# A reshape, tile and logsumexp kernel: the x buffers moved by 96 bytes, to a multiple of 4096

## The chip, the cores and the metric

The kernel runs on one core of a Trainium2 chip. Such a core has five engines with instruction streams of their own: TensorE (PE) for matmuls, VectorE (DVE), ScalarE (ACT), GpSimd (POOL) and SyncE (SP), which here issues transfers. Sixteen DMA engines move data between DRAM and the core's on-chip memory, which has 128 partitions. The metric is the time of one execution on the device in microseconds, as the median of several runs.

## What is computed

The input x has the shape (8, 2048, 2048) in float32, 134 MB. Its last dimension is cut into 8 heads of 256 columns. A bias of 256 values per head is added, and the logarithm of the sum of exponentials is taken over each head's 256 columns. Each result stands twice in the output, of shape (8, 8, 4096).

```python
def reference(x, bias):
    B, S, D = x.shape
    H = bias.shape[0]
    Dh = D // H
    x_heads = x.reshape(B, S, H, Dh).transpose(0, 2, 1, 3)
    x_heads = x_heads + bias[None, :, None, :]
    x_tiled = np.repeat(x_heads, 2, axis=2)
    mx = x_tiled.max(axis=-1, keepdims=True)
    lse = mx.squeeze(-1) + np.log(np.exp(x_tiled - mx).sum(axis=-1))
    return lse.astype(np.float32)
```

## The kernel before

x is worked through in 64 tiles of 256 rows of the sequence: 128 partitions with K = 2 rows of 2048 columns each, 2 MB a tile. The kernel takes exponentials without subtracting a maximum first; at the end a small judgement over all sums decides whether a slower loop (`all_again`) is needed, which runs only for extreme data.

**Buffers.** All tiles of on-chip memory come out of one pool, `sb`, which hands out places in the order in which the code asks for them, each at a multiple of 32 bytes (lines 155 to 201). First come the bias and its copies, among them `b_rep` (line 156, the bias of heads 4 to 7 in every partition) and `w_sb` (line 157), then the sums `R`, then the results `res`, `res_two` and `res_last` (lines 195 to 200), and last the four buffers `xb0` to `xb3` (line 201). Each of the four holds KB = 4 rows of 2048 float32 per partition, 32,768 bytes. `xts` (line 202) cuts them into eight places for a tile.

**Loads.** SP issues all loads of x, in the order of the program. The first two tiles come one by one (line 276). Tiles 2 to 41 come in pairs, one transfer of 4 MB into a whole buffer, in which each partition receives 32 KB in one piece (line 261). From tile 42 on each tile has its own transfer again, with 16 KB in one piece per partition, or 8 KB in the last batch, where a partition's two rows lie apart in DRAM. Tiles from 57 on are loaded row by row, 1 MB each, and the last two tiles in ten parts of 1 to 8 heads (`TAIL_LOADS`, line 54). A load into a buffer waits for the last uses of what stood there (`last_uses`, collected per tile); `reload` (line 289) issues it.

**Work on a tile.** Most tiles go by the split `BULK`. PE adds the bias to heads 0 to 2 (line 464: x times the identity on top of the bias in PSUM), and ACT takes their exponentials from there (lines 475 and 482). POOL adds the bias to heads 4 to 7 in place (line 514, `g_add`), ACT takes the exponentials of heads 3 to 7 (line 520), and DVE multiplies head 3 by the exponential of its bias (line 532) and sums all heads but the first in one reduction (line 539). The last tiles use other splits, and the last two follow an order written out by hand (`TAIL`, line 71): there PE adds the bias per piece (line 846) and runs small matmuls between (line 455) whose results aren't used. The order of the instructions on every engine is that of the program; no scheduler moves them.

The functions that the change touches are printed here; it stands among the tiles of the kernel's own function.

Of the kernel before, what the change touches and what calls it, by code (L numbers as in the profile page):

```python
# [9 lines left out]
F32 = mybir.dt.float32  # L10
# [114 lines left out]
def kernel(  # L125
# [7 lines left out]
    P = nc.NUM_PARTITIONS  # L133
# [16 lines left out]
    sb = ctx.enter_context(tc.tile_pool(name="sb", bufs=1))  # L150
# [47 lines left out]
    ]  # L198
    res_two = sb.tile([H * NBLK, P, K, 2], F32, name="res_two")
    res_last = sb.tile([P, P, 2], F32, name="res_last")  # L200
    xbs = [sb.tile([P, KB, D], F32, name=f"xb{i}") for i in range(NBUF // TB)]
    xts = [xb[:, k : k + K] for xb in xbs for k in range(0, KB, K)]
    w_ps = pp.tile([P, W2 - W0], F32, name="w_ps")
# [100 lines left out]
    for set_idx, (_name, funcs) in enumerate(get_activation_tables(nc.m.arch).items()):  # L304
        if ACT.Exp in funcs and ACT.Ln in funcs:
            nc.scalar.add_instruction(
                mybir.InstLoadActFuncSet(
                    name=nc.get_next_instruction_name(),
# [707 lines left out]
```

## Time and profile before

| | |
|---|---|
| median of 3 runs | 325.6 us (325.59 to 325.68) |
| the profiled execution's own time | 325.55 us |
| its span, from the first to the last instruction | 323.7 us |
| granted TensorE clock, mean | 0.961 |
| read from DRAM, written | 134.23 MB, 1.05 MB |
| DMA packets | 8806 |

The span is shorter than the execution by what lies before the first and after the last instruction. In the rows over time the span is cut into 40 equal slices, and each digit is a busy share in tenths. A row of a group reads: line, engine, operation, what it writes and reads with shapes, the count, then busy time in us and the mean of one in ns, then the engine's idle time just before, and what ended it. In the rows of a DMA queue stand packets, MB, and the time that the packets took as a share of the 16 DMA engines' time; rows of single transfers give their size in KB and the median time from issue to landing.

### The profile page before, as it was taken

The numbers are of one execution on the slowest core, as the hardware profiler recorded it, in microseconds if no ns is written. First come the engines' busy times: TensorE is split into PE (matmuls) and PEld (weight loads), VectorE is DVE, ScalarE is ACT, GpSimd is POOL, SyncE is SP. The second block draws the span as 40 slices with busy tenths as digits, with TensorE's granted clock in tenths as the row PEclk, the third lists the DMA queues.
The fourth block names the chain that finished last, engine by engine and source line by source line (L and its number), as shares of the span: only waits on it lengthen the run. The fifth ranks groups of instructions, "written<-read, shape, count | busy, mean of one in ns | idle before, by whom it ended". The sixth has DMA issues, their size and how long they took to land.

```text
span 323.7 us, 2296 instructions
## 1 busy us (share of the span) xinstructions
PE 247.5 (76%) x619; PEld 100.1 (31%) x620; DVE 288.0 (89%) x310; ACT 265.6 (82%) x436; POOL 287.9 (89%) x119
## 2 busy tenths in 40 slices
PE   5997787688776698886668878677778678688775
PEld 1332332233332233332223323233233322233333
DVE  1339998889999969999999998999999999989985
ACT  1169868878778869688889869878988999999995
POOL 7949997999999999999999999999999999878783
PEclk9999979899999879799999979999999999799999
DMA  7999999999999999999999999999999999999993
GB/s 309 470 397 445 454 401 440 445 409 441 445 409 442 441 407 441 441 413 438 445 410 441 441 411 441 413 427 427 433 429 422 429 424 426 419 421 419 419 399 145
DMA packets 8806, 135.44 MB, mean 418 GB/s; under 512 B 980, under 2 KB 1239, under 8 KB 2519
## 3 DMA queue, kind: packets, MB, share of 16 engines
q1 hardware_dynamic: 8640, 135.14, 98.2%
q10 hardware_dynamic: 152, 0.14, 0.1%
q8 instruction: 5, 0.08, 0.1%
q14 instruction: 9, 0.07, 0.1%
HBM read 134.23 MB, written 1.05 MB: 418 GB/s over the span
## 4 chain that ended last, share of the span: by engine, by line
DMA 58%; POOL 18%; ACT 14%; PE 5%; DVE 3%; SPq 1%; issue 0%
DMA xb<-in_x_dram 58%; POOL xb L514 18%; ACT xb L520 9%; DVE R L539 2%; PE pair L464 2%; ACT xb L495 2%; ACT xb L482 1%; PE one_ps L464 1%; ACT xb L475 1%; PE pair L846 1%; PE tp L455 1%; SPq L261 1%; DVE xb L532 0%; SPq L276 0%; PE pair L826 0%
## 5 line engine op out<-in xcount | busy, mean ns | idle before, releaser
L514 POOL TENSOR_TENSOR xb<-xb,b_rep 128x2048 f32<-128x2048 f32 x57 | 256.7, 4527 | 21.2 <-DMA xb<-in_x_dram 21.2
L539 DVE TENSOR_REDUCE R<-xb 128x14 f32<-128x3584 f32 (+1 forms) x57 | 216.8, 3803 | 3.4 <-ACT xb L520 1.5
L520 ACT ACTIVATE xb<-xb 128x2560 f32<-128x2560 f32 (+5 forms) x80 | 156.2, 1965 | 20.1 <-POOL xb L514 19.5
L464 PE MATMUL pair<-xb,ident 128*128 128x512 f32 x216 | 108.2, 625 | 0.0
L464 PE MATMUL one_ps<-xb,ident 128*128 128x512 f32 x108 | 62.9, 667 | 20.2 <-DMA xb<-in_x_dram 20.2
L482 ACT ACTIVATE xb<-pair 128x1024 f32<-128x1024 f32 x54 | 55.3, 1025 | 17.4 <-PE pair L464 17.3
L464 PEld LDWEIGHTS pair<-xb,ident 128*128 128x128 f32 x216 | 44.1, 204 | 58.1 <-issue 58.1
L532 DVE TENSOR_TENSOR xb<-xb,w_ps 128x512 f32<-128x512 f32 x54 | 36.7, 680 | 21.2 <-ACT xb L520 21.2
L406 PE MATMUL one_ps<-b,ones_bf 128*128 128x512 bf16 x52 | 19.9, 382 | 38.0 <-ACT xb L475 38.0
L475 ACT ACTIVATE xb<-one_ps 128x256 f32<-128x256 f32 x108 | 39.8, 375 | 6.8 <-PE one_ps L464 6.8
L406 PEld LDWEIGHTS <-ones_bf 128*128 128x128 bf16 (+1 forms) x174 | 17.3, 100 | 85.4 <-issue 78.5
L406 PE MATMUL pair<-b,ones_bf 128*128 128x512 bf16 x104 | 31.0, 379 | 0.0
L464 PEld LDWEIGHTS one_ps<-xb,ident 128*128 128x128 f32 x108 | 19.6, 200 | 35.7 <-DMA xb<-in_x_dram 29.8
L441 PE MATMUL pair<-xb,ident 128*128 128x512 f32 x32 | 18.6, 684 | 8.5 <-DMA xb<-in_x_dram 8.5
L555 DVE CUSTOM_DVE_ANT_0 xb<-xb,w_ps 128x256 f32<-128x256 f32 x60 | 22.1, 413 | 0.4 <-ACT xb L520 0.4
L475 ACT ACTIVATION_READ_ACCUMULATOR xb<-one_ps 128x1 f32 x108 | 21.8, 202 | 0.0
L578 POOL TENSOR_TENSOR xb<-xb 128x128 f32<-128x128 f32 (+3 forms) x36 | 13.5, 379 | 2.5
L495 ACT ACTIVATE xb<-pair 128x256 f32<-128x256 f32 x38 | 14.4, 395 | 1.0 <-PE pair L846 0.7
L572 POOL TENSOR_TENSOR xb<-xb,w_sb 128x256 f32<-128x256 f32 (+1 forms) x12 | 10.1, 840 | 4.3 <-ACT xb L520 3.7
L455 PE MATMUL tp<-b_rep,ident 128*128 128x384 f32 x30 | 12.0, 486 | 0.0
L441 PEld LDWEIGHTS pair<-xb,ident 128*128 128x128 f32 x32 | 5.3, 197 | 17.7 <-DMA xb<-in_x_dram 15.9
L495 ACT ACTIVATION_READ_ACCUMULATOR xb<-pair 128x1 f32 x38 | 8.4, 220 | 0.0
(66 smaller groups left out, 84.0 us busy)
## 6 DMA issues: line engine op xcount, KB each, us to landing
xb<-in_x_dram SPq DMA_DIRECT2D x20, 4096.0 KB, 22.6
xb<-in_x_dram SPq DMA_DIRECT2D x17, 2048.0 KB, 22.7
xb<-in_x_dram SPq DMA_DIRECT2D x11, 1024.0 KB, 22.8
xb<-in_x_dram SPq DMA_DIRECT2D x5, 256.0 KB, 9.9
xb<-in_x_dram SPq DMA_DIRECT2D x2, 512.0 KB, 17.6
xb<-in_x_dram SPq DMA_DIRECT2D x1, 640.0 KB
out_dram<-res SPq DMA_DIRECT2D x1, 512.0 KB
out_dram<-res SPq DMA_DIRECT2D x1, 256.0 KB, 5.5
```

Source lines behind the costliest of these rows:

```text
L406: nc.tensor.matmul(p, lhsT=lhsT, rhs=each_row(b, h * Dh, Dh, K), start=i == 0, stop=False,)
L441: mm = nc.tensor.matmul(p, lhsT=ident, rhs=xts[t % NBUF][:, ka:kb, c : c + w], start=False, stop=True,)
L455: nc.tensor.matmul(tp[:, 0 : WARM // P], lhsT=ident, rhs=b_rep[:, 0:WARM], start=True, stop=True)
L464: mm = nc.tensor.matmul(p, lhsT=ident, rhs=xts[t % NBUF][:, :, h * Dh : (h + 1) * Dh], start=False, stop=True,)
L475: act = nc.scalar.activation(out=xts[t % NBUF][:, k, 0:Dh], in_=got[0][:, k * Dh : (k + 1) * Dh], func=ACT.Exp, accum_out=sums[:, k, 0:1],)
L482: act = nc.scalar.activation(out=xts[t % NBUF][:, :, Dh : m["pe"] * Dh].rearrange("p k (h j) -> p h k j", j=Dh), in_=got[-1].rearrange("p ...
L495: act = nc.scalar.activation(out=xts[t % NBUF][:, k, h * Dh : (h + 1) * Dh], in_=p, func=ACT.Exp, accum_out=sums[:, k, h : h + 1],)
L514: add = nc.gpsimd.tensor_tensor(out=v, in0=v, in1=each_row(b_rep, c - G0, D - c, k1 - k0), op=ALU.add)
L520: return on_x(t, nc.scalar.activation(out=v, in_=v, func=ACT.Exp), [after])
L532: mul = nc.vector.tensor_tensor(out=f, in0=f, in1=each_row(w_ps, m["pe"] * Dh - W0, n, k1 - k0), op=ALU.mult,)
L539: red = nc.vector.tensor_reduce(out=sums[:, k0:k1, h0:H], in_=v.rearrange("p k (h j) -> p k h j", j=Dh), op=ALU.add, axis=mybir.AxisListTy ...
L555: ttr = nc.vector.tensor_tensor_reduce(out=v, in0=v, in1=w, scale=1.0, scalar=0.0, op0=ALU.mult, op1=ALU.add, accum_out=dst,)
```

## The change

A tile of 24 float32, 96 bytes per partition, is asked of the pool between `res_last` and the x buffers. Nothing writes or reads it.

```diff
     res_two = sb.tile([H * NBLK, P, K, 2], F32, name="res_two")
     res_last = sb.tile([P, P, 2], F32, name="res_last")
+    sb.tile([P, 24], F32, name="gap")
     xbs = [sb.tile([P, KB, D], F32, name=f"xb{i}") for i in range(NBUF // TB)]
     xts = [xb[:, k : k + K] for xb in xbs for k in range(0, KB, K)]
```

In the built programs `res_last` stays at byte 60,320 of each partition, and the four buffers, 32,768 bytes apart, begin at byte 61,440 in place of 61,344. All other tiles stay where they were. The order of the instructions on each engine, their shapes and their waits are the same; the lines after 200 count one higher.

## The prediction

> **What bounds the kernel now.** I read first the page's head, with the busy time of each engine, and the rows over time for the DMA engines.
>
> ```profile
> span 323.7 us, 2296 instructions
> ...
> PE 247.5 (76%) x619; PEld 100.1 (31%) x620; DVE 288.0 (89%) x310; ACT 265.6 (82%) x436; POOL 287.9 (89%) x119
> ...
> DMA  7999999999999999999999999999999999999993
> GB/s 309 470 397 445 454 401 440 445 409 441 445 409 442 441 407 441 441 413 438 445 410 441 441 411 441 413 427 427 433 429 422 429 424 426 419 421 419 419 399 145
> ...
> q1 hardware_dynamic: 8640, 135.14, 98.2%
> ```
>
> No compute engine is above 89%, while the queue that loads x keeps the 16 DMA engines busy for 98.2% of the span. From the second slice to the last but one the DMA row stands at 9. The rate sinks a little towards the end, from some 430 to 420 GB/s; that slope is used below. Next come the chain of work that ended last and the DMA queue's own waits.
>
> ```profile
> DMA 58%; POOL 18%; ACT 14%; PE 5%; DVE 3%; SPq 1%; issue 0%
> ```
>
> ```profile
> SPq L261 <- DVE R L539: 177.1, 17, 27.2
> ```
>
> The loads hold 58% of the chain. SP waits 177.1 us for VectorE to free buffers, but that wait costs nothing as long as earlier transfers in the queue fill the DMA engines, and the DMA row says they do. The chain gives 18% to POOL, so I compared POOL's own pace with the loads'.
>
> ```profile
> L514 POOL TENSOR_TENSOR xb<-xb,b_rep 128x2048 f32<-128x2048 f32 x57 | 256.7, 4527 | 21.2 <-DMA xb<-in_x_dram 21.2
> L539 DVE TENSOR_REDUCE R<-xb 128x14 f32<-128x3584 f32 (+1 forms) x57 | 216.8, 3803 | 3.4 <-ACT xb L520 1.5
> ```
>
> A tile of x is 2,097,152 bytes; at the 431 GB/s measured below it takes 4.87 us to arrive. POOL's addition takes 4.53 us a tile and is itself kept waiting by the loads for 21.2 us in all. So the DMA engines set the pace and POOL has 7% in hand. Last, the end of the chain in order of time:
>
> ```profile
> 299.82 14.39 DMA xb<-in_x_dram
> 314.21 0.04 issue
> 314.26 0.70 PE pair L846 x2
> ...
> 320.81 0.15 DVE verdict L681
> ```
>
> The work after the last awaited load begins at 314.26 us and has 9.4 us to the span's end. It is short work on landed data, so it moves with the stream: a microsecond saved on the loads is a microsecond saved at the end.
>
> **The change, part by part.** It adds a tile that no instruction names: no instruction, no DMA, no wait. The order on every engine stays. The buffers of x move from byte 61,344 of each partition to byte 61,440, which is 15 times 4096. The old start lies 160 bytes past a multiple of 256 and 96 bytes short of one of 4096; the four buffers are 32,768 bytes apart, so all share this offset. Two costs could change: the DMA engines' time for a row, and the compute engines' time on x.
>
> **The DMA engines' time for a row.** Each partition's contiguous run is one packet, as the counts show: the loads have these sizes,
>
> ```profile
> xb<-in_x_dram SPq DMA_DIRECT2D x20, 4096.0 KB, 22.6
> xb<-in_x_dram SPq DMA_DIRECT2D x17, 2048.0 KB, 22.7
> xb<-in_x_dram SPq DMA_DIRECT2D x11, 1024.0 KB, 22.8
> xb<-in_x_dram SPq DMA_DIRECT2D x5, 256.0 KB, 9.9
> xb<-in_x_dram SPq DMA_DIRECT2D x2, 512.0 KB, 17.6
> xb<-in_x_dram SPq DMA_DIRECT2D x1, 640.0 KB
> ...
> xb<-in_x_dram SPq DMA_DIRECT2D x1, 128.0 KB, 14.4
> ```
>
> and 57 loads of 128 rows, with 128 more because tile 56 takes two separate rows per partition, make 7,424 rows: 464 for each of the 16 engines. Three stretches of the DMA view hold rows of one length each, 32, 16 and 8 KB: 20 to 200 us, 218 to 262 us and 277 to 300 us, in this order.
>
> ```profile
> DMA packets 2675, 77.55 MB, mean 431 GB/s; under 512 B 304, under 2 KB 304, under 8 KB 304
> q1 hardware_dynamic: 2668, 77.46, 100.1%
> ```
>
> ```profile
> DMA packets 1294, 18.85 MB, mean 428 GB/s; under 512 B 143, under 2 KB 143, under 8 KB 143
> q1 hardware_dynamic: 1292, 18.83, 100.6%
> ```
>
> ```profile
> DMA packets 1317, 9.68 MB, mean 421 GB/s; under 512 B 135, under 2 KB 135, under 8 KB 135
> q1 hardware_dynamic: 1316, 9.68, 101.3%
> ```
>
> The packets under 512 B mark completions; the rest of q1's are rows. The engines are full throughout, so a row costs 16 engines times the stretch over its rows: 16 x 180 / 2364 = 1.2183 us, 16 x 44 / 1149 = 0.6127 us, 16 x 23 / 1181 = 0.3116 us. Doubling the row from 16 to 32 KB adds 0.6056 us, which is 27.06 bytes per ns; from 8 to 16 KB it adds 0.3011 us, or 27.2. What doesn't grow with length is 2 x 0.6127 - 1.2183 = 7.1 ns by the longer pair and 2 x 0.3116 - 0.6127 = 10.5 ns by the shorter, with each row's share of completions in it. Over 464 rows that is 3.3 to 4.9 us. Alignment can act on this part alone, so 4.9 us bounds a gain: 320.7 us.
>
> How much of it comes from the odd start? No row shows a load into an aligned buffer. The nearest row is the last store, alone on the DMA engines at the end (321 to 323.7 us). It writes rows of 1 KB to DRAM, not to a row of x.
>
> ```profile
> q10 hardware_dynamic: 144, 0.13, 14.3%
> ...
> out_dram<-res_last ACTq DMA_DIRECT2D x1, 128.0 KB, 1.8
> ```
>
> Its 128 rows and 16 completions took 14.3% of 16 x 2.7 us, or 6.18 us; the bytes account for 131,072 / 27.06 = 4.84 us, and 1.33 us over 144 packets is 9.3 ns each. Counted the same way, completions included, the loads' 7.1 to 10.5 ns a row (9 packets per 8 rows) are 6.3 to 9.3 ns a packet. Loads begin oddly where they write and the store begins oddly where it reads (its source, res_last, lies at byte 60,320, also 160 past a multiple of 256); both have the same fixed time. So a fixed time of this size belongs to any packet, and I take nothing for the odd start. Bounds: a gain of 4.9 us as above; on the other side the nearest row is again the fixed part, paid once more if aligned rows were treated worse, 3.3 us at its lower value, 328.9 us.
>
> [...]
>
> **The compute engines' time on x.** PE, ACT, DVE and POOL do the same instructions 96 bytes further on. The loads hide them: POOL's 4.53 us stands under 4.87 us. If that cover went, each per cent on POOL's addition beyond the 7% would cost 0.045 x 57 = 2.6 us. No row shows the addition at another offset; the nearest is POOL's small subtraction on other tiles:
>
> ```profile
> L327 POOL TENSOR_TENSOR brest<-brow,bparts 1x768 f32<-1x768 f32 x1 | 1.6, 1627 | 0.1
> ```
>
> It takes 1627 / 768 = 2.12 ns an element against 4527 / 2048 = 2.21 for the addition, at unlike offsets. A move of 4% between offsets stays under the cover. I take nothing.
>
> **Sum.** The profiled execution took 325.55 us, 1.85 us of it outside the span; the median of the three runs is 325.6. With zero for both terms, 325.55 stays, and beside the median 325.6 us.
>
> **Rivals.** First, the odd start does cost on the write side: the piece of 160 bytes in front of every row is carried as if it were data. For it: 160 / 27.06 = 5.9 ns fits inside the fixed 7.1 to 10.5 ns. Against it: the store, and that it would leave only 1.2 ns at the lower value for all else. Its price is 464 x 5.9 ns = 2.7 us, 322.9 us; the stream would still be the bound, since a gain of 0.9% doesn't use up POOL's 7%. [...]
>
> Second, a smaller piece goes away: one broken-up write per row, priced by the unexplained spread of the fixed part, 10.5 - 7.1 = 3.4 ns, 1.6 us in all: 324.0 us. For it stands that something in the fixed part differs between stretches; against it, that the stretches have the same offset.
>
> Third, on the other side: with all rows beginning on the same boundary, the writes of the 16 engines and the accesses of the compute engines to x fall on the same pieces of memory more often. Its place is the row, its price 0.46 us for each ns a row; it decides (passes 0.65 us) from 1.4 ns, and at the spread of 3.4 ns it gives 327.2 us. For it: the rate already varies between slices, from 397 to 454 GB/s in the first ten. Against it: the buffers have a common offset now as well. [...]
>
> Fourth, the change does nothing because the buffers don't move: the placement in the built program excludes it, so it adds only to no change.
>
> **How the numbers follow.** No change 0.45 (with the fourth), the 160 bytes 0.18, the smaller piece 0.15, the collisions 0.22. A difference of 0.2%, 0.65 us, is about what a measurement here can tell from none. So faster 0.33, same 0.45, slower 0.22. The likeliest case's own range is 325.0 to 326.2; the range that takes in both signs runs from 322.6, just under the first rival, to 327.2.
>
> **What would show it.** Right: the rates of the three stretches stay at 431, 428 and 421 GB/s, the addition at 4527 ns, the last awaited load at 314.2 us. First rival: a row costs 5.9 ns less in every stretch, so that the 8 KB stretch reaches 429 GB/s and the 32 KB one 432.5. Third: those rates fall, most for short rows. I am wrong if the time moves with the rates unchanged, for then the start or the tail made it, or if POOL's addition passes 4.87 us.

## The result, and the profile after

The changed kernel takes 323.6 us (323.49 to 323.71 over 6 runs) beside 325.63 us for the kernel before (325.59 to 325.78, 6 runs). The ratio is 0.9937 with an interval of 0.9924 to 0.9950: 2.0 us faster. The time lies inside the range that was given, which took in both signs; the direction, no change, was not right.

The page's head, the rows over time of the DMA engines and the group of POOL's addition, for the changed kernel:

```profile
span 321.8 us, 2297 instructions
...
PE 249.2 (77%) x620; PEld 101.1 (31%) x620; DVE 287.5 (89%) x310; ACT 264.4 (82%) x436; POOL 288.9 (90%) x119
...
DMA  7999999999999999999999999999999999999993
...
q1 hardware_dynamic: 8640, 135.14, 98.2%
...
L515 POOL TENSOR_TENSOR xb<-xb,b_rep 128x2048 f32<-128x2048 f32 x57 | 257.6, 4549 | 19.1 <-DMA xb<-in_x_dram 19.1
```

The DMA engines are full as before and for the same 98.2% of a span that is 1.9 us shorter, with the same packets and bytes. The compute engines do what they did; POOL's addition is 4549 ns in place of 4527. So the DMA engines got through the same rows sooner. The end of the chain in order of time:

```profile
298.26 14.05 DMA xb<-in_x_dram
312.31 0.04 issue
312.36 0.70 PE pair L847 x2
```

The work after the last awaited load begins at 312.36 us, it was 314.26: the whole 1.9 us is there when the last load lands, and the tail behind it is as long as it was. The chain's shares changed more than the time (DVE has 27% of it now, it had 3%). With SP waiting for VectorE (177.5 us at L262, 79.9 us at L277) as well as for transfers (28.2 us at L277), the chain can go back through either; the DMA row says that the engines stayed full all along (9 from the second slice to the last but one).

The three stretches of the DMA view with rows of 32, 16 and 8 KB, 20 to 200 us, 218 to 262 us and 277 to 300 us:

```profile
DMA packets 2684, 77.84 MB, mean 432 GB/s; under 512 B 304, under 2 KB 304, under 8 KB 304
q1 hardware_dynamic: 2677, 77.76, 100.1%
```

```profile
DMA packets 1304, 19.00 MB, mean 432 GB/s; under 512 B 144, under 2 KB 144, under 8 KB 144
q1 hardware_dynamic: 1302, 18.97, 100.8%
```

```profile
DMA packets 1339, 9.81 MB, mean 427 GB/s; under 512 B 141, under 2 KB 141, under 8 KB 141
q1 hardware_dynamic: 1338, 9.81, 101.0%
```

By the prediction's own arithmetic a row now costs 16 x 180 / 2373 = 1.2137 us, 16 x 44 / 1158 = 0.6079 us and 16 x 23 / 1197 = 0.3074 us: 4.6, 4.8 and 4.2 ns less than before, whatever the row's length. Over the 464 rows of an engine that makes 1.9 to 2.2 us, which is the gain.

The trace also records how long each packet took, though not on which engine; where rows of an engine are counted below, they are a sixteenth of all. These are the commonest durations of the load queue's rows, in ns with their counts, and the mean, before and after (counted from the trace's packets):

```
rows of 32 KB  before  1213 x657, 1214 x548, 1218 x389, 1221 x338   mean 1217.5
               after   1213 x2543 of 2560                          mean 1214.1
rows of 8 KB   before  311 x471, 314 x246, 312 x154, 313 x137       mean 314.3
               after   309 x1661 of 1664                            mean 309.3
```

Before, a row took its shortest time or some ns more, in several steps; after, nearly every row takes the shortest time. The changed kernel's stream has lost a spread that for most rows was 0 to 12 ns. From about its 6th row to its 31st each engine takes the shortest time before the change too. The experiments ask what boundary the price hangs on, whose it is, and why these first rows don't pay it. Below, a row is called odd when its start in on-chip memory is not a multiple of 256 bytes, and even when it is.

### The profile page after: what moved, and what is told of

Read it like the earlier page. It is cut to its first block, busy times and chain, and to the rows that moved or that the text cites. A ratio compares the mean times of both kernels' runs of the same rounds, so it can differ in the third digit from the quotient of the medians.

```text
span 321.8 us, 2297 instructions
## 1 busy us (share of the span) xinstructions
PE 249.2 (77%) x620; PEld 101.1 (31%) x620; DVE 287.5 (89%) x310; ACT 264.4 (82%) x436; POOL 288.9 (90%) x119
## 3 DMA queue, kind: packets, MB, share of 16 engines
q1 hardware_dynamic: 8640, 135.14, 98.2%
## 4 chain that ended last, share of the span: by engine, by line
DMA 54%; DVE 27%; PE 6%; ACT 6%; POOL 4%; SPq 1%; issue 0%
DMA xb<-in_x_dram 54%; DVE R L540 23%; ACT xb L521 4%; POOL xb L515 4%; DVE xb L533 4%; PE pair L465 3%; PE one_ps L465 2%; ACT xb L483 1%; PE pair L847 1%; PE tp L456 1%; DVE R L635 1%; ACT xb L476 0%; SPq L262 0%; SPq L277 0%; PE pair L827 0%
## 5 line engine op out<-in xcount | busy, mean ns | idle before, releaser
L515 POOL TENSOR_TENSOR xb<-xb,b_rep 128x2048 f32<-128x2048 f32 x57 | 257.6, 4549 | 19.1 <-DMA xb<-in_x_dram 19.1
L465 PE MATMUL pair<-xb,ident 128*128 128x512 f32 x216 | 110.2, 636 | 0.0
L465 PEld LDWEIGHTS pair<-xb,ident 128*128 128x128 f32 x216 | 45.0, 208 | 59.0 <-issue 59.0
L442 PE MATMUL pair<-xb,ident 128*128 128x512 f32 x32 | 18.4, 676 | 8.0 <-DMA xb<-in_x_dram 7.9
L442 PEld LDWEIGHTS pair<-xb,ident 128*128 128x128 f32 x32 | 5.4, 196 | 16.6 <-DMA xb<-in_x_dram 14.8
```

The costliest lines, as they stand in the source:

```text
L442: mm = nc.tensor.matmul(p, lhsT=ident, rhs=xts[t % NBUF][:, ka:kb, c : c + w], start=False, stop=True,)
L465: mm = nc.tensor.matmul(p, lhsT=ident, rhs=xts[t % NBUF][:, :, h * Dh : (h + 1) * Dh], start=False, stop=True,)
L515: add = nc.gpsimd.tensor_tensor(out=v, in0=v, in1=each_row(b_rep, c - G0, D - c, k1 - k0), op=ALU.add)
```

## Experiments

### Which boundary

Against the changed kernel, only the size of the unused tile differs, so that x begins 32 bytes short of a multiple of 64, and on odd multiples of 64, 128 and 256.

```diff
-    sb.tile([P, 24], F32, name="gap")
+    sb.tile([P, 16], F32, name="gap")   # start_32; 40, 56 and 88 columns in the other three
```

> The x buffers begin at byte 61,408, 32 bytes short of a multiple of 64 (and of 4096). Theory A (a row that doesn't begin on some boundary pays a few ns more on its DMA engine): 325.3 to 325.9 us, the rates of the 32, 16 and 8 KB stretches as before the change (431, 428, 421 GB/s). Rival B (it is the move that counts, away from a chance collision between x and the other tiles, not the boundary): near 323.6 us.

> The x buffers begin at byte 61,504, a multiple of 64 and not of 128. Theory A with a boundary of 64 bytes: 323.6 us, the 8 KB stretch at 427 GB/s. Theory A with a boundary of 128 or more: 325.6 us and 421 GB/s. Rival B (a chance collision of places): anything between 323.6 and 325.6 us, out of order with the other starts.

> The x buffers begin at byte 61,568, a multiple of 128 and not of 256. Theory A with a boundary of 64 or 128 bytes: 323.6 us; with a boundary of 256 or more: 325.6 us. Rival C (the boundary is 4096, as the change has it): 325.6 us.

> The x buffers begin at byte 61,696, a multiple of 256 and not of 512. Theory A with a boundary of at most 256 bytes: 323.6 us, packets of 8 KB rows as in the changed kernel, 8 KB stretch at 427 GB/s. Rival C (the boundary is 4096): 325.6 us and 421 GB/s.

| start | past a multiple of 256 by | us, median | ratio to before, interval |
|---|---|---|---|
| 61,408 | 224 | 326.18 | 1.0013, 1.0004 to 1.0023 |
| 61,504 | 64 | 325.75 | 1.0002, 0.9992 to 1.0012 |
| 61,568 | 128 | 325.65 | 0.9996, 0.9986 to 1.0005 |
| 61,696 | 0 | 323.72 | 0.9941, 0.9924 to 0.9957 |

The 8 KB stretch (277 to 300 us) of the start at 128 and of the one at 256:

```profile
q1 hardware_dynamic: 1317, 9.68, 101.3%
```

```profile
q1 hardware_dynamic: 1338, 9.81, 101.1%
```

A multiple of 128 gains nothing, a multiple of 256 has the full gain. The 4096 in the change's name is not needed, and theory A holds with a boundary of 256 bytes. Rival B, a chance collision with other tiles, would not sort these starts. What I hadn't put in any expectation is the first row of the table: 224 bytes past a boundary is a little slower than the 160 of the kernel before (8 KB rows: mean 315.1 ns against 314.3).

### The loads alone

A kernel of its own brings x in through four buffers in rows of 8 KB, 1024 rows for each DMA engine. Sums, exponentials and the output's values are left out. Its loop, shortened:

```python
for i in range(B * n):
    xb = xbs[i % 4]
    nc.sync.dma_start(out=xb, in_=rows)    # rows: x[b, 512 rows] as "(k p) d -> p k d"
    nc.vector.tensor_copy(seen[:, i : i + 1], xb[:, 0, 0:1])
```

> Loads alone: x is brought in through four buffers at byte 61,344 and so on, all in rows of 8 KB, and of each load one column is copied so that the buffer is used before it is filled again; sums, exponentials and the output's values are left out (zeros are written). Theory A1 (the price is the DMA engines' own): a row costs 3 to 6 ns more than in the run with buffers at 61,440, over 1024 rows an engine 3 to 6 us, some 320 against 316 us. Theory A2 (odd rows collide with the compute engines' accesses to x, for which these are gone): no difference within 0.5 us.

> The same loads alone into buffers at byte 61,440 and so on. Both theories: the 8 KB rows go at 427 GB/s, as in the changed kernel's 8 KB stretch, some 316 us. A1: 3 to 6 us below the run with odd buffers; A2: within 0.5 us of it.

With buffers at 61,344 it took 328.27 us, with buffers at 61,440 it took 323.76 us, one run each. The absolute times were expected 8 us too low (I had counted the rows' own time and little else); the difference, 4.5 us, is within what A1 said. The DMA view from 20 to 300 us, odd buffers and then even:

```profile
DMA packets 14873, 118.17 MB, mean 422 GB/s; under 512 B 448, under 2 KB 448, under 8 KB 448
q1 hardware_dynamic: 14873, 118.17, 101.4%
```

```profile
DMA packets 15101, 119.91 MB, mean 428 GB/s; under 512 B 464, under 2 KB 464, under 8 KB 464
q1 hardware_dynamic: 15101, 119.91, 101.0%
```

14,425 and 14,637 rows in 280 us are 310.6 and 306.1 ns a row: 4.5 ns for an odd start. VectorE was busy for 2% of this span and PE and ACT not at all, so the price is no collision with the compute engines' accesses.

In this run, too, the first rows are free. In the trace's packets the price sets in near row 38 of each engine, some 14 us after the start; in the kernel before it sets in near row 42, some 43 us after the start, since most of its rows there are four times as long. Between these two runs it is the count of rows that agrees, not the time.

### Half of the buffers

Against the changed kernel, the four buffers are asked for one by one, with 160 unused bytes between the second and the third (the lines that matter):

```diff
+        if i == 2:
+            sb.tile([P, 40], F32, name="gap2")
         xbs.append(sb.tile([P, KB, D], F32, name=f"xb{i}"))
```

> Buffers xb0 and xb1 begin on a multiple of 256, xb2 and xb3 160 bytes past one, as all four did before. Theory A (every row with an odd start pays its own price): half of the gain, 324.6 us, and two kinds of rows side by side. Rival D (one odd stream disturbs all, so that the DMA engines lose step with each other): little of the gain, 325.2 to 325.7 us.

324.35 us, ratio 0.9959 (0.9945 to 0.9973): 70% of the gain, by the time nearest to theory A. But the rows don't bear A out. The 8 KB stretch stands at the full rate although half of its buffers are odd:

```profile
q1 hardware_dynamic: 1337, 9.81, 101.1%
```

and of the 2560 rows of 32 KB, 2441 take the shortest 1213 ns, where half of them should have been slower. Neither theory had said so: odd rows among even ones are nearly free. Most of what was still paid lies in the last part, where tiles 62 and 63 are loaded in pieces into `xb3` alone, an odd buffer (the 5 KB rows take 200.5 ns on average, as before, against 196.0 in the changed kernel). What the packets took beyond the shortest times adds up to some 0.4 us an engine more than in the changed kernel, of the 0.7 us between the two kernels. Together with the free first rows this suggested some slack in each DMA engine that takes up the price of some 40 odd rows and is given back by even ones. The next run was made for that.

> Loads alone as before, but two buffers begin 160 bytes past a multiple of 256 and two on one, so that each DMA engine gets 64 odd rows of 8 KB, then 64 even ones, and so on; sums, exponentials and the output's values are left out. In the run with odd buffers alone the first 37 rows or so of each engine cost nothing and all later ones some 5.5 ns. Theory S (an odd row's price is first taken up by some slack in the engine, and even rows give the slack back): prices only in the second half of each odd run, 324.4 to 325.2 us. Theory P (each odd row pays for itself): half of the way between the two runs, 326.0 us. Theory D (once the engines have lost step, odd rows pay from then on): 325.8 to 326.0 us, with clean rows in even runs alone.

Against the loads alone with odd buffers (the lines that matter):

```diff
+        if i == 2:
+            sb.tile([P, 24], F32, name="gap")
         xbs.append(sb.tile([P, KB, D], F32, name=f"xb{i}"))
```

324.93 us (one run), inside what theory S gave and 1 us below the other two. The DMA view of this run from 4 to 12 us (odd rows, early), 92 to 100 us (odd rows, late in a run of 64) and 62 to 90 us (even rows and the first odd ones after):

```profile
DMA packets 416, 3.41 MB, mean 426 GB/s; under 512 B 0, under 2 KB 0, under 8 KB 0
...
DMA packets 413, 3.38 MB, mean 423 GB/s; under 512 B 0, under 2 KB 0, under 8 KB 0
...
DMA packets 1498, 12.00 MB, mean 429 GB/s; under 512 B 33, under 2 KB 33, under 8 KB 33
```

In the packets of the same run nearly all rows from 62 to 90 us take 309 ns, and from 92 to 100 us most take 311 to 321 ns; this pattern comes back with each turn through the buffers. After the first turn some 32 of the 64 odd rows are free each time. So slack is the reading that foretold the number. What the slack is made of no run shows.

### Which side, which end

Loads alone again, into even buffers, with rows cut to 8032 bytes, so that a row has one broken piece of 96 bytes beside 31 whole blocks of 256.

```diff
-        nc.sync.dma_start(out=xb, in_=rows)
+        nc.sync.dma_start(out=xb[:, :, 0:2008], in_=rows[:, :, 40:2048])   # cols_src
```

(`cols_00` reads columns 0 to 2007 and writes them there; `cols_both` reads and writes 40 to 2047.)

> Loads alone, rows cut to 8032 bytes, read from the start of each 8 KB row in DRAM and written to the start of an even row: starts even on both sides, ends odd. The last 40 columns of each row and all of the arithmetic are left out. If ends cost nothing: 160 bytes less for each of 1024 rows an engine is 6.0 us below the 323.8 us of whole even rows, 317.7 us. If an odd end costs like an odd start: about 322 us.

> The same, read from 160 bytes into each row in DRAM, written to an even start; the first 40 columns and the arithmetic are left out. Theory W (only the written start counts): as the run with even starts on both sides. [...] Theory M (read and written starts must match modulo 256): 4 to 6 us more.

> The same with both starts 160 bytes past a multiple of 256; the first 40 columns and the arithmetic are left out. Theory W: 4.5 us more than the run with even starts on both sides, as whole odd rows stand to whole even ones. [...] Theory M: no more than it.

They took 320.69, 320.57 and 320.75 us, one run each: all alike, and 3 us above the 317.7 us that was worked out for rows without a price. An odd read start alone (`cols_src`) cost nothing against the other two, and theory M falls, since starts that differ were no dearer than starts that match. Theory W falls in the form I had given it, for it expected 4.5 us between the last and the first. What the three have in common is one broken block a row where they write, at its end or at its start. Their rows from 20 to 300 us, the same in all three within three packets:

```profile
q1 hardware_dynamic: 15247, 118.74, 101.3%
```

The reads were broken at one end at least in all of them, so one thing stayed open, and two runs settled it: rows of 31 whole blocks, written whole, and read either from the row's start or from 160 bytes into it.

```diff
+        nc.sync.dma_start(out=xb[:, :, 0:1984], in_=rows[:, :, 40:2024])   # blocks_src; 0:1984 in blocks_even
```

> Loads alone, rows cut to 7936 bytes, 31 blocks of 256, even starts and ends on both sides; the last 64 columns and the arithmetic are left out. No broken block anywhere: 256 bytes less for each of 1024 rows an engine is 9.6 us below whole even rows, 314.1 us, and no slower rows late in the run.

> The same, but read from 160 bytes into each row in DRAM, so that reads begin and end inside a block and writes don't; 64 of the columns and the arithmetic are left out. Theory W (only broken writes cost): 314.1 us as the other. Theory R (an odd read start carries the 160 bytes in front): 6.0 us more. Reads priced like writes: 4.5 us more.

314.21 and 313.97 us, one run each, where 314.1 was expected of both if only broken writes cost. A price for the second run's reads of 6.0 us (theory R) or of 4.5 us doesn't show. From 20 to 300 us, reads from a row's start and then from inside it:

```profile
q1 hardware_dynamic: 15579, 119.83, 101.2%
```

```profile
q1 hardware_dynamic: 15581, 119.84, 101.2%
```

Broken reads from DRAM are free here: 313.97 us against 314.21. (No trace shows where x begins in DRAM; the two reads lie 160 bytes apart, so at least one of them starts inside a block.) Broken writes into on-chip memory cost 2.8 ns for one piece of 96 bytes a row (320.69 us against 317.8, which is 314.21 us plus 96 bytes at 27.06 bytes per ns for 1024 rows, over 1024 rows) and 4.5 ns for the two pieces, 96 and 160 bytes, that an odd row of whole blocks breaks into.

One estimate fits both prices, though no run was made to test it: each block that a row touches where it writes costs a fixed 4.5 ns beside the time of its bytes. An odd row of 8 KB touches 33 blocks in place of 32 and pays 4.5 ns more. A cut row touches 32 blocks for the bytes of 31.375, and 0.625 x 4.5 = 2.8 ns. It also fits the starts at 64 and 128, which cost as much as 160, but not the slightly dearer one at 224.

The cut rows, too, are free at first. In `cols_00` and `cols_both` the price sets in only between rows 50 and 60 of each engine. A price of 2.8 ns fills the slack later than one of 4.5: 55 x 2.8 = 154 ns against 38 x 4.5 = 171 ns, so the slack is, by this estimate, some 150 to 170 ns of an engine's time.

### The stores as well

```diff
+    sb.tile([P, 24], F32, name="gap")
     res = [
```

> The 96 bytes lie in front of the result tiles in place of the x buffers: x begins at 61,440 as in the changed kernel, and the result tiles begin on multiples of 256 too. Theory A for stores as well as loads: 323.5 us or up to 0.1 less than the changed kernel, and the last store's rows cheaper by some ns. Rival (only where SBUF is written): 323.6 us, the last store as before at 14% of its stretch.

323.65 us, ratio 0.9935 (0.9919 to 0.9952): the same as the changed kernel, and no better. The last store, over the last 2.7 us of the span, took 14.3% of the DMA engines' time in the changed kernel and here

```profile
q10 hardware_dynamic: 144, 0.13, 13.9%
```

which is 1.2 ns a packet. The packets' times show more than this sum does. In all seven profiles of the whole kernel in which `res_last` lies at byte 60,320, 160 past a multiple of 256, the last store's 128 rows take 44 to 58 ns, 46.9 to 47.4 on average. Here, with `res_last` on a multiple of 256, 113 of them take 46 ns and 15 take 44, 45.8 on average. So an odd start does cost this store, which reads on-chip memory, between 1.1 and 1.6 ns a row, as far as one profile with an even start can say; for eight rows on each engine that is 0.01 us. The earlier stores' rows of 4 KB show no such price: in the changed kernel, where they too are read from odd starts, every row of 4 KB takes 159 ns.

## Why the prediction was right or wrong

The range ran from 3 us below to 1.6 us above the forecast, so that the time lies in it says little for the working. Its parts are judged one by one.

**What bounds the kernel: right.** The DMA engines set the pace, the gain of 1.9 us was complete when the last load landed, and it came through to the end undiminished. POOL's 7% of slack wasn't used up.

**The compute engines' time on x: right.** POOL's addition moved by 22 ns, and stayed under the loads.

**The DMA engines' time for a row: wrong, and this is the step that failed.** The prediction found a fixed time of 7.1 to 10.5 ns in the loads and of 9.3 ns in the last store, and concluded: "So a fixed time of this size belongs to any packet, and I take nothing for the odd start." The comparison could not carry that. The fixed time is a small difference between large numbers: done again on the changed kernel it gives 2 x 0.6079 - 1.2137 = 2.1 ns and 2 x 0.3074 - 0.6079 = 6.9 ns. The loads' values fell by 5.0 and 3.6 ns, while the two pairs of one kernel differ by 3.4 and 4.8 ns, so the method is uncertain by as much as it was to find. The store was also no fair stand-in: it reads on-chip memory where the loads write it, and its own odd start cost it 1.2 ns a packet, not 4 to 5. That the two fixed times came out alike was chance. And the store has 8 rows an engine, where the loads' price sets in after some 40. In place of the nothing that was taken, the runs show 4.2 to 4.8 ns for each row that is written from an odd start: 1.9 to 2.2 us.

**The first rival: right in kind, mis-sized.** It named the written side, a price for each row, and a stream that remains the bound. Its 5.9 ns, for 160 bytes carried in vain, no run shows: measured were 4.2 to 4.8 ns a row, and 2.0 us in place of 2.7. Its reason is not the right one: at 27.06 bytes per ns a start 64 bytes past a boundary would then pay 2.4 ns and one at 128 would pay 4.7, but both kernels took as long as the one at 160 (325.75 and 325.65 us beside 325.7). And the rows of `cols_00`, written from even starts, paid 2.8 ns for the 96 bytes by which they end past a boundary, with no bytes in front of their start.

**The second rival** put its 1.6 us on "one broken-up write per row", which at 3.4 ns a row is near the 2.8 ns that the cut rows show, but drew the size from the spread between stretches, which was noise of the method.

**The third rival fell** in every run that tested it: starts on a boundary made the rows faster (8 KB rows: mean 309.3 ns in place of 314.3), and with VectorE busy for 2% of the span and PE and ACT idle the odd rows still paid 4.5 ns. The varying rate that was to speak for it says nothing: from the second slice to the tenth it runs from 397 to 470 GB/s before (454, as the prediction had it, is not the highest) and from 399 to 467 after.

## What to carry to other kernels

Where the DMA engines are the bound, as they are here with 98.2% of the span, let every row that is loaded begin and end on a multiple of 256 bytes in on-chip memory; a multiple of 4096 gave no more (323.6 us against 323.72). The price was paid per row, so short rows lost most: 4.6 ns is 0.4% of a row of 32 KB, and 4.5 ns is 1.5% of one of 8 KB. And before a fixed cost is read out of the rates of two stretches, the same arithmetic on a second pair shows how much of it is noise.

## What the runs showed that I had not expected

Odd rows are free for a while: the first 38 rows of each engine in the loads alone, and nearly all of them in runs of 16 between even ones (2441 of 2560 rows of 32 KB at the shortest 1213 ns). A test of these loads with fewer than 38 rows on each engine would have found nothing.

A broken block costs the loads only where it is written: 2.8 ns for one piece of 96 bytes a row, 4.5 for the two pieces of an odd row, nothing for reads from DRAM (313.97 us against 314.21). The last store, which reads on-chip memory from an odd start, pays as well, 1.1 to 1.6 ns a row as far as one profile with an even start shows.
